# Grouped 3x3 convolution: one weight tile, a longer lag between two pipes, and an early write into the output

## The chip, the cores and the metric

One core of one Trainium2 chip. The metric is the device time of one execution in microseconds (us), as the median of several runs. The profile is of one execution.

## The reference

`x` is 16 x 64 x 64 x 64 (batch, channels, height, width), `weight` is 128 x 8 x 3 x 3, both fp32, with 8 groups. Each group takes 8 input channels to 16 output channels with a 3x3 kernel and zero padding of 1; the output is 16 x 128 x 64 x 64 in fp32.

```python
for g in range(groups):
    for b in range(batch):
        for co in range(16):
            for ci in range(8):
                for kh in range(3):
                    for kw in range(3):
                        output[b, g*16 + co] += weight[g*16 + co, ci, kh, kw] * \
                            x_pad[b, g*8 + ci, kh:kh+h, kw:kw+w]
```

## The kernel before

**Data.** The 16 x 64 rows (image, channel) of `x` are read in tiles of 128 rows, two images in each. Four tiles `xn0` to `xn3` hold images 0 to 7. Four tiles `xs0` to `xs3` hold images 8 to 15 shifted by 32 rows, so that in `xs` the 32-row blocks of an image stand at other partitions than in `xn`. All of them are bf16. They are loaded by 17 DMAs which GpSimd issues at the start, with a cast from fp32 on the way (`load`, L105). Only rows 0 to 31 of `xn0` come another way: SyncE reads them as fp32 into `raw`, which is the first half of the last output buffer (L116), and ScalarE casts them in two pieces (L121).

**Weights.** `weight` lands in `w_sb` (L118, issued by ScalarE). GpSimd makes a mask of groups and an identity (L136 to L146). VectorE multiplies weights and mask into `E` (5 products, L162); TensorE transposes `E` by 18 products with the identity (L175), 9 with offset 0 and 9 with offset 32; VectorE copies the first nine into `wN`, ScalarE the others into `wS` (L185). A 32x64 piece of these tiles is the block-diagonal weight of four groups for one tap of the 3x3 kernel.

**Two pipes.** Pipe 0 works on `xn` with `wN`, pipe 1 on `xs` with `wS`. Each has 16 sets (`st`): for each of four pairs of images `i`, four sets `s` of 16 image rows. A set has 9 taps; each tap is 8 matmuls of a 32x64 piece of the array (L240), for two images, two halves of the channels and two banks. The first tap is the middle one, the others follow in their order. The order of instructions is written out over slots: a pipe takes one tap in a slot, then rests 3 slots after 9 (`PERIOD` 12). Pipe 1 runs `LAG` 6 slots behind pipe 0, so that always at least one of them has a tap.

**Out.** After a set, `finish` copies four PSUM banks into two output buffers `ob` (L268; ScalarE and VectorE in turn). There are eight buffers of 2 MB, one image in each; a pair of images takes two, pipes in turn, so a pair uses the buffers that the same pipe's pair `i - 2` had, and its first copy waits for that one's stores (`self.empty`). SyncE issues the stores (L278): after the last set of a pair, whole images of 2 MB; for the first pair of both pipes (`i == 0`), halves of 1 MB, one after set 1 and one after set 3.

Of the kernel before, what the change touches and what calls it, by code (L numbers as in the profile page):

```python
# [7 lines left out]
FP32 = mybir.dt.float32  # L8
BF16 = mybir.dt.bfloat16
ALU = mybir.AluOpType  # L10


@with_exitstack
def kernel(
    ctx: ExitStack,
    tc: tile.TileContext,
    x: bass.AP,
    weight: bass.AP,
    groups: int,
    out: bass.AP,  # L20
):
    nc = tc.nc

    B, C, H, W = x.shape
    CO, CIg, K, _ = weight.shape
    G = groups
    COg = CO // G
    HW = H * W
    T = K * K
    assert (B, C, CO, K, G, H, W) == (16, 64, 128, 3, 8, 64, 64)  # L30

    R = 8
    NCH = H // R
    HALF = HW // 2

    NOB = 8

    pool = ctx.enter_context(tc.tile_pool(name="sb", bufs=1))
    psum = ctx.enter_context(tc.tile_pool(name="psum", bufs=1, space=bass.MemoryType.PSUM))

    xn = [pool.tile([128, H, W], BF16, name=f"xn{i}") for i in range(4)]
    xs = [pool.tile([128, H, W], BF16, name=f"xs{i}") for i in range(4)]
    ob = [pool.tile([128, HW], FP32, name=f"ob{i}") for i in range(NOB)]
    w_sb = pool.tile([128, CIg * T], FP32, name="w_sb")
    mask = pool.tile([128, G], FP32, name="mask")
    ident = pool.tile([128, 128], BF16, name="ident")
    E = pool.tile([128, T, 160], BF16, name="E")
    wN = pool.tile([128, T, 128], BF16, name="wN")
    wS = pool.tile([128, T, 128], BF16, name="wS")
    banks = [psum.tile([128, 512], FP32, name=f"bank{i}") for i in range(8)]  # L50

    with tc.tile_critical():  # L52
        program(nc, x, weight, out, xn, xs, ob, w_sb, mask, ident, E, wN, wS, banks)


class Order:
# [23 lines left out]
        return self.sem, self.n  # L80


def program(nc, x, weight, out, xn, xs, ob, w_sb, mask, ident, E, wN, wS, banks):
    H = W = 64
    HW, HALF, T, G, CIg, COg, R = H * W, H * W // 2, 9, 8, 8, 16, 8
    NOB = len(ob)
# [7 lines left out]
    def sem(name):  # L94
        s = nc.alloc_semaphore(name)
        sems.append(s)
        return s
# [13 lines left out]
                landed[t.name, q, h] = (s, 16)  # L111


    raw = ob[NOB - 1][:, 0:HALF]
    s_raw = sem("raw")
    nc.sync.dma_start(raw, xr[0:128, 0:HALF]).then_inc(s_raw, 16)  # L116
    s_w = sem("w")
    nc.scalar.dma_start(w_sb, weight.rearrange("co ci kh kw -> co (ci kh kw)")).then_inc(s_w, 16)  # L118
    ACT.wait((s_raw, 16))
    for h in (0, 16):  # L120
        raw_read = ACT.done(nc.scalar.copy(  # L121
            xn[0][:, h : h + 16, :].rearrange("p h w -> p (h w)"), raw[:, h * W : (h + 16) * W],
        ))
        for q in range(4):
            for r in range(h, h + 16):
                landed[xn[0].name, q, r] = raw_read

    m1 = DVE.done(nc.vector.memset(mask, 1.0))  # L128
    m2 = DVE.done(nc.vector.memset(ident, 0.0))  # L129
    for h0, h1 in ((0, 32), (32, 64)):  # L130
        if h0 > 0:
            load(xn[0], 0, 0, 128, h0, h1)
        load(xs[0], 544, 0, 128, h0, h1)
        if h0 == 0:
            POOL.wait(m1)
            m3 = POOL.done(nc.gpsimd.affine_select(  # L136
                out=mask, in_=mask, compare_op=ALU.is_ge, fill=0.0,
                base=0, channel_multiplier=1, pattern=[[-COg, G]],
            ))
            POOL.wait(m2)  # L140
            m4 = POOL.done(nc.gpsimd.affine_select(  # L141
                out=ident, in_=ident, compare_op=ALU.not_equal, fill=1.0,
                base=0, channel_multiplier=1, pattern=[[-1, 128]],
            ))
            POOL.wait(m3)
            m5 = POOL.done(nc.gpsimd.affine_select(  # L146
                out=mask, in_=mask, compare_op=ALU.is_ge, fill=0.0,
                base=COg - 1, channel_multiplier=-1, pattern=[[COg, G]],
            ))
        load(xs[3], 512 - 96, 96, 128, h0, h1)  # L150
    for i in range(1, 4):
# [3 lines left out]

    wv = w_sb.rearrange("co (ci t) -> co t ci", t=T)
    DVE.wait((s_w, 16), m5)
    for r in range(5):  # L160
        g0 = 4 * (r % 2)
        e = DVE.done(nc.vector.tensor_mul(  # L162
            E[:, :, 32 * r : 32 * r + 32].rearrange("p t (g c) -> p t g c", c=CIg),
            wv.unsqueeze(2).to_broadcast([128, T, 4, CIg]),
            mask[:, g0 : g0 + 4].unsqueeze(1).unsqueeze(3).to_broadcast([128, T, 4, CIg]),
        ))
    PE.wait(e, m4)
    free = [None] * 8
    w_need = {}
    for k, (wt, off) in enumerate(((wN, 0), (wS, 32))):  # L170
        for g, t0 in enumerate(range(0, T, 4)):
            n = min(4, T - t0)
            b = 4 * k + g
            for t in range(n):
                ins = nc.tensor.matmul(  # L175
                    banks[b][:, 128 * t : 128 * t + 128],
                    E[:, t0 + t, off : off + 128],
                    ident,
                    start=True, stop=True,
                )  # L180
            p = PE.done(ins)
            dst = wt[:, t0 : t0 + n, :].rearrange("p t c -> p (t c)")
            eng, copy = ((DVE, nc.vector.tensor_copy), (ACT, nc.scalar.copy))[k]
            eng.wait(p)
            free[b] = eng.done(copy(dst, banks[b][:, 0 : 128 * n]))  # L185
            for t in range(n):
                w_need[wt.name, t0 + t] = free[b]

    outf = out.rearrange("b co h w -> b co (h w)")
    taps = [(1, 1)] + [(a, b) for a in range(3) for b in range(3) if (a, b) != (1, 1)]
    pe = nc.tensor
    stored = [nc.alloc_semaphore(f"st{i}") for i in range(NOB)]
    uses = [0] * NOB
    nob = [0]
# [2 lines left out]
    class Pipe:  # L200
# [5 lines left out]
        def streams(self, i):  # L206

            if self.k == 0:
                return [(q // 2, wN, xn[i], q, q % 2) for q in range(4)]
            return [  # L210
                (0, wS, xs[i], 0, 1), (1, wS, xs[i], 1, 0),
                (1, wS, xs[i], 2, 1), (0, wS, xs[i - 1], 3, 0),
            ]

        def matmuls(self, st, k, j):
# [6 lines left out]
            v0 = w0 - (kw - 1)  # L222
            nr, nw = hi - lo, w1 - w0
            left = {0: 2, 1: 2}
            for im, wt, xt, q, half in self.streams(i):
                b = self.banks[j][im]
                pos = dict(tile_position=(32 * q, 64 * half))
                w_ap = wt[32 * q : 32 * q + 32, 3 * kh + kw, 64 * half : 64 * half + 64]
                x_ap = xt[32 * q : 32 * q + 32, lo:hi, w0:w1]
                o_ap = banks[b].rearrange("p (h w) -> p h w", w=W)[  # L230
                    64 * half : 64 * half + 64, o0 : o0 + nr, v0 : v0 + nw
                ]
                if j == 0:
                    PE.wait(w_need[wt.name, 3 * kh + kw])
                    pe.ldweights(w_ap, **pos)  # L235
                PE.wait(
                    free[b] if k == 0 else None,
                    landed[xt.name, q, lo], landed[xt.name, q, hi - 1],
                )
                ins = pe.add_instruction(  # L240
                    mybir.InstMatmult(
                        name=nc.get_next_instruction_name(),
                        engine=mybir.EngineType.PE,
                        start_tensor_calc=k == 0, stop_tensor_calc=k == T - 1,
                        tile_size=(32, 64), ldweights=False, **pos,
                        ins=[pe.lower_ap(x_ap, opt=False), pe.lower_ap(w_ap, opt=False, for_matmul_weights=True)],
                        outs=[pe.lower_ap(o_ap)],
                    )
                )
                left[im] -= 1  # L250
                if k == T - 1 and left[im] == 0:
                    self.full[j, im] = PE.done(ins)

        def finish(self, st):
            i, s = st // 4, st % 4
            if s == 0:
                self.slots = [(nob[0] + im) % NOB for im in range(2)]
                self.empty = [(stored[slot], 16 * uses[slot]) if uses[slot] else raw_read for slot in self.slots]
                self.wrote = [[], []]
                nob[0] += 2  # L260
            for j in range(2):
# [7 lines left out]
                    self.wrote[im].append(free[b])  # L269
                nev[0] += 1  # L270
            nev[0] += 1
            if s == 1 and i == 0 or s == 3:
                o0, o1 = (0 if s == 1 or not (i == 0) else HALF), HALF * (s + 1) // 2
                for im in range(2):
                    slot = self.slots[im]
                    img = 2 * i + 8 * self.k + im
# [2 lines left out]
                    uses[slot] += 1  # L279

    pipes = (Pipe(0), Pipe(1))
    PERIOD, LAG, NSETS = T + 3, (T + 3) // 2, 16
    for slot in range(PERIOD * NSETS + LAG):
        live = []
        for p, lag in zip(pipes, (0, LAG)):
# [60 lines left out]
```

## Time and profile before

| | |
|---|---|
| median of 10 runs | 128.52 us (128.32 to 128.94) |
| the profiled execution, own time | 128.49 us |
| its span (first to last recorded event) | 126.8 us |
| TensorE matmul busy | 87.1 us (69%) |
| VectorE, ScalarE, GpSimd busy | 46.0, 39.0, 9.9 us |
| bytes read from and written to memory | 16.81 MB, 33.55 MB |
| stores of an image, of a half | 12 of 2048 KB, 8 of 1024 KB |

The span leaves out 1.7 us of the execution's own time. In a table of windows, a row is a stretch of the span: its bounds, its length, each engine's busy time, the TensorE clock, the DMA share (mean busy share of the 16 DMA engines, over 1 where packets of two queues overlap on an engine) and the GB/s that landed. A load with a cast counts there with the bf16 bytes that it writes, which is half of what it reads.

### The profile page before, as it was taken

The page shows a single profiled execution, that of the slowest core. Times are in us where ns is not written, and L with a number is a line of the kernel's source. Part 1 is how long each engine was busy: PE and PEld are TensorE (multiplying, and loading weights), DVE is VectorE, ACT ScalarE, POOL GpSimd, SP SyncE. Part 2 cuts the span into 40 slices and gives each one's busy share as a digit, 9 for nine tenths or more (in the row PEclk, how much of TensorE's full clock was granted, in tenths as well). Part 3 has the DMA queues.
Part 4 walks back from the last instruction along what each step waited for, and adds up shares of the span by engine and source line. Part 5 has one row for each costly group of instructions (what it writes and reads, how often), then busy time and mean ns, then how long its engine had stood idle before and what let it go on. Part 6 is the DMA issues. An engine that isn't in the chain of part 4 may idle for free.

```text
span 126.8 us, 3785 instructions
## 1 busy us (share of the span) xinstructions
PE 87.1 (69%) x2322; PEld 39.9 (31%) x1170; DVE 46.0 (36%) x74; ACT 39.0 (31%) x70; POOL 9.9 (8%) x24
## 2 busy tenths in 40 slices
PE   0029999999999999997539999999999700000000
PEld 0024435445444554551114446443363200000000
DVE  0273065456445544444224654555446500000000
ACT  4063153345335433341033633426335400000000
POOL 5995000000000000000000000000000000000000
PEclk9999999999999999999999999999999995555555
DMA  2999999999999999999999999999999999999960
GB/s 47 349 209 208 220 213 207 211 282 310 319 314 308 330 302 321 318 313 314 408 426 421 429 434 424 419 429 424 424 429 424 424 429 445 424 429 439 419 279 10
DMA packets 5375, 42.74 MB, mean 337 GB/s; under 512 B 752, under 2 KB 752, under 8 KB 2672
## 3 DMA queue, kind: packets, MB, share of 16 engines
q1 hardware_dynamic: 3024, 34.60, 65.2%
q0 software_dynamic: 2192, 7.87, 31.1%
q8 instruction: 13, 0.21, 0.6%
q10 hardware_dynamic: 144, 0.04, 0.2%
q14 instruction: 2, 0.02, 0.0%
HBM read 16.81 MB, written 33.55 MB: 397 GB/s over the span
## 4 chain that ended last, share of the span: by engine, by line
PE 45%; DMA 27%; DVE 5%; issue 1%; ACT 0%; SPq 0%; ACTq 0%; DVEq 0%
PE bank L240 44%; DMA out_dram<-ob 24%; DMA w_sb<-in_weight_dram 4%; DVE ob L268 3%; DVE E L162 2%; PE bank L175 2%; ACT ob L268 0%; ACTq L341 0%; DVEq L74 0%; SPq L278 0%; SPq L52 0%
## 5 line engine op out<-in xcount | busy, mean ns | idle before, releaser
L240 PE MATMUL bank<-xs,wS 32*64 32x504 bf16 (+3 forms) x1152 | 72.0, 373 | 3.6 <-ACT ob L268 1.9
L240 PE MATMUL bank<-xn,wN 32*64 32x504 bf16 (+3 forms) x1152 | 71.2, 377 | 1.1 <-DVE ob L268 1.1
L268 DVE COPY ob<-bank 128x512 f32<-128x512 f32 x64 | 41.4, 686 | 49.4 <-PE bank L240 41.7
L268 ACT COPY ob<-bank 128x512 f32<-128x512 f32 x64 | 34.5, 589 | 55.4 <-PE bank L240 45.6
L235 PEld LDWEIGHTS <-wS 32*64 32x64 bf16 x576 | 26.2, 104 | 23.6 <-issue 13.8
L235 PEld LDWEIGHTS <-wN 32*64 32x64 bf16 x576 | 19.3, 105 | 27.7 <-issue 23.0
L175 PE MATMUL bank<-ident,E 128*128 128x128 bf16 x18 | 2.1, 310 | 8.6 <-DVE E L162 8.6
L105 POOL DMA_DIRECT2D xs<-in_x_dram x10 | 5.9, 591 | 1.0 <-SPq L52 1.0
L175 PEld LDWEIGHTS bank<-ident,E 128*128 128x128 bf16 x18 | 1.8, 143 | 8.6 <-DVE E L162 8.6
L162 DVE TENSOR_TENSOR E<-w_sb,mask 128x288 bf16<-128x288 f32 x5 | 2.9, 651 | 4.4 <-DMA w_sb<-in_weight_dram 4.4
L105 POOL DMA_DIRECT2D xn<-in_x_dram x7 | 4.2, 601 | 0.0
L121 ACT CAST xn<-ob 128x1024 bf16<-128x1024 f32 x2 | 2.0, 1044 | 3.9 <-DMA ob<-in_x_dram 3.9
L185 ACT CAST wS<-bank 128x512 bf16<-128x512 f32 (+1 forms) x3 | 1.2, 487 | 1.7 <-PE bank L175 1.7
L185 DVE CAST wN<-bank 128x512 bf16<-128x512 f32 (+1 forms) x3 | 1.5, 551 | 0.7 <-PE bank L175 0.7
L121 ACT ACT_TABLE_LOAD x1 | 1.3, 1283 | 1.4 <-SPq L52 1.4
L128 DVE MEMSET mask<- 128x8 f32 x1 | 0.1, 65 | 1.1 <-SPq L52 1.1
L141 POOL TENSOR_SCALAR_AFFINE_SELECT ident<-ident 128x128 bf16<-128x128 bf16 x1 | 0.3, 304 | 0.0
L136 POOL TENSOR_SCALAR_AFFINE_SELECT mask<-mask 128x8 f32<-128x8 f32 x1 | 0.2, 211 | 0.1
L146 POOL TENSOR_SCALAR_AFFINE_SELECT mask<-mask 128x8 f32<-128x8 f32 x1 | 0.2, 199 | 0.0
L327 POOL MEMSET const-float32-0.0<- 128x1 f32 x1 | 0.1, 99 | 0.3 <-issue 0.3
L129 DVE MEMSET ident<- 128x64 uint32 x1 | 0.1, 112 | 0.0
L327 POOL MEMSET const-bfloat16-1.0<- 128x1 bf16 x1 | 0.1, 103 | 0.0
(2 smaller groups left out, 0.2 us busy)
## 6 DMA issues: line engine op xcount, KB each, us to landing
out_dram<-ob SPq DMA_DIRECT2D x12, 2048.0 KB, 19.9
out_dram<-ob SPq DMA_DIRECT2D x8, 1024.0 KB, 21.9
xn<-in_x_dram POOLq DMA_DIRECT2D x7, 512.0 KB, 24.0
xs<-in_x_dram POOLq DMA_DIRECT2D x6, 512.0 KB, 17.2
ob<-in_x_dram SPq DMA_DIRECT2D x1, 1024.0 KB, 5.5
xs<-in_x_dram POOLq DMA_DIRECT2D x2, 384.0 KB, 49.0
xs<-in_x_dram POOLq DMA_DIRECT2D x2, 128.0 KB, 9.1
w_sb<-in_weight_dram ACTq DMA_DIRECT2D x1, 36.0 KB, 4.7
```

Source lines behind the costliest of these rows:

```text
L105: nc.gpsimd.dma_start(t.rearrange("p h w -> p (h w)")[p0:p1, h0 * W : h1 * W], xr[row0 + p0 : row0 + p1, h0 * W : h1 * W],).then_inc(s, 16)
L121: raw_read = ACT.done(nc.scalar.copy(xn[0][:, h : h + 16, :].rearrange("p h w -> p (h w)"), raw[:, h * W : (h + 16) * W],))
L136: m3 = POOL.done(nc.gpsimd.affine_select(out=mask, in_=mask, compare_op=ALU.is_ge, fill=0.0, base=0, channel_multiplier=1, pattern=[[-COg, ...
L141: m4 = POOL.done(nc.gpsimd.affine_select(out=ident, in_=ident, compare_op=ALU.not_equal, fill=1.0, base=0, channel_multiplier=1, pattern=[ ...
L146: m5 = POOL.done(nc.gpsimd.affine_select(out=mask, in_=mask, compare_op=ALU.is_ge, fill=0.0, base=COg - 1, channel_multiplier=-1, pattern= ...
L162: e = DVE.done(nc.vector.tensor_mul(E[:, :, 32 * r : 32 * r + 32].rearrange("p t (g c) -> p t g c", c=CIg), wv.unsqueeze(2).to_broadcast([ ...
L175: ins = nc.tensor.matmul(banks[b][:, 128 * t : 128 * t + 128], E[:, t0 + t, off : off + 128], ident, start=True, stop=True,)
L185: free[b] = eng.done(copy(dst, banks[b][:, 0 : 128 * n]))
L235: pe.ldweights(w_ap, **pos)
L240: ins = pe.add_instruction(mybir.InstMatmult(name=nc.get_next_instruction_name(), engine=mybir.EngineType.PE, start_tensor_calc=k == 0, st ...
L268: free[b] = eng.done(copy(ob[slot][:, o0 : o0 + 512], banks[b]))
L327: nc = _bacc.Bacc("TRN2", target_bir_lowering=False, num_devices=1)
```

## The change

1. One weight tile `wt` takes the place of `wN` and `wS`. VectorE first spreads the weights over all 16 blocks of 8 columns in `wb` (3 copies), TensorE transposes (9 products), and VectorE multiplies by a mask of 128x4 on the way out of PSUM (3 products). The mask is built as 128x4x4 and summed to 128x4 by one reduction. The taps come in another order: 4, 5, 6, 7, 0, 1, 2, 3, 8.
2. `raw` is read in two DMAs (image rows 0 to 7, then 8 to 31) and cast in four pieces of 8 rows.
3. ScalarE issues one more DMA at the start: 16 rows of 512 B of `x` are written into output image 15. That image is overwritten later; SyncE waits for this DMA ahead of its first store.
4. Pipe 1 runs 18 slots behind pipe 0, not 6.
5. Of the first pairs, only pipe 0's is stored in halves; pipe 1's is stored as whole images.

```diff
-    raw = ob[NOB - 1][:, 0:HALF]
-    s_raw = sem("raw")
-    nc.sync.dma_start(raw, xr[0:128, 0:HALF]).then_inc(s_raw, 16)
+    raw = ob[NOB - 1]
     s_w = sem("w")
     nc.scalar.dma_start(w_sb, weight.rearrange("co ci kh kw -> co (ci kh kw)")).then_inc(s_w, 16)
-    ACT.wait((s_raw, 16))
-    for h in (0, 16):
-        raw_read = ACT.done(nc.scalar.copy(
-            xn[0][:, h : h + 16, :].rearrange("p h w -> p (h w)"), raw[:, h * W : (h + 16) * W],
-        ))
...
+    s_warm = sem("warm")
+    outf = out.rearrange("b co h w -> b co (h w)")
+    nc.scalar.dma_start(outf[15][0:16, 0:128], xr[0:16, 0:128]).then_inc(s_warm, 16)
+    raw_read = []
+    for h0, h1 in ((0, 8), (8, 32)):
+        s_raw = sem(f"raw{h0}")
+        nc.sync.dma_start(raw[:, h0 * W : h1 * W], xr[0:128, h0 * W : h1 * W]).then_inc(s_raw, 16)
+        for h in range(h0, h1, 8):
+            ACT.wait((s_raw, 16))
+            raw_read = [ACT.done(nc.scalar.copy(
+                xn[0][:, h : h + 8, :].rearrange("p h w -> p (h w)"), raw[:, h * W : (h + 8) * W],
+            ))]
...
+    taps = [(t // 3, t % 3) for t in (4, 5, 6, 7, 0, 1, 2, 3, 8)]
+    DVE.wait(m5)
+    r = DVE.done(nc.vector.tensor_reduce(
+        out=mask, in_=mask4.rearrange("p q g -> p g q"), op=ALU.add, axis=mybir.AxisListType.X,
+    ))
+    DVE.wait((s_w, 16))
     wv = w_sb.rearrange("co (ci t) -> co t ci", t=T)
-    DVE.wait((s_w, 16), m5)
-    for r in range(5):
-        g0 = 4 * (r % 2)
-        e = DVE.done(nc.vector.tensor_mul(
...
+    groups = ((0, 4, 4), (4, 0, 4), (8, 8, 1))
+    filled = [DVE.done(nc.vector.tensor_copy(
+        wb[:, k0 : k0 + n, :].rearrange("p t (g c) -> p t g c", c=CIg),
+        wv[:, t0 : t0 + n, :].unsqueeze(2).to_broadcast([128, n, 16, CIg]),
+    )) for k0, t0, n in groups]
+    PE.wait(m4)
+    free = [None] * 8
+    w_need = []
+    for b, (k0, t0, n) in enumerate(groups):
+        PE.wait(filled[b])
+        for k in range(n):
+            ins = nc.tensor.matmul(
+                banks[b][:, 128 * k : 128 * k + 128], wb[:, k0 + k, :], ident, start=True, stop=True,
+            )
+        p = PE.done(ins)
+        DVE.wait(p, r)
+        free[b] = DVE.done(nc.vector.tensor_mul(
+            wt[:, k0 : k0 + n, :].rearrange("p t (h g c) -> p (t h) g c", h=2, g=4),
+            banks[b][:, 0 : 128 * n].rearrange("p (t g c) -> p t g c", g=4, c=COg),
+            mask.unsqueeze(1).unsqueeze(3).to_broadcast([128, 2 * n, 4, COg]),
         ))
...
+        w_need += [free[b]] * n
...
+    SP.wait((s_warm, 16))
...
-            if s == 1 and i == 0 or s == 3:
-                o0, o1 = (0 if s == 1 or not (i == 0) else HALF), HALF * (s + 1) // 2
+            if s == 1 and i + self.k == 0 or s == 3:
+                o0, o1 = (0 if s == 1 or not (i + self.k == 0) else HALF), HALF * (s + 1) // 2
...
-    PERIOD, LAG, NSETS = T + 3, (T + 3) // 2, 16
+    PERIOD, LAG, NSETS = T + 3, (T + 3) // 2 + T + 3, 16
```

## The prediction

> **What bounds the kernel now.** I read the page's slices first, then its list of DMA issues, then the waits, then a table of windows.
>
> ```profile
> PE   0029999999999999997539999999999700000000
> PEclk9999999999999999999999999999999995555555
> DMA  2999999999999999999999999999999999999960
> ```
>
> The DMA engines are busy from the second slice to the last but one; TensorE stops at about 101 us and 25 us of stores follow. So TensorE is not the end's cause. The waits say the same:
>
> ```profile
> ACT ob L268 <- DMA out_dram<-ob: 9.9, 3, 6.6
> DVE ob L268 <- DMA out_dram<-ob: 7.7, 3, 3.6
> PE bank L240 <- DVE ob L268: 2.6, 4, 1.5
> PE bank L240 <- ACT ob L268: 1.9, 1, 1.9
> ```
>
> The copies out of PSUM wait for stores (second figure: times), and TensorE waits for those copies. No row has a matmul waiting for an `xn` or `xs` load. The windows then give the rate of the DMA engines, stage by stage (last column GB/s landed):
>
> ```profile
> 2.00:3.00 1.00, 0.00 (x0) 0.00 (x0) 0.00 (x0) 0.69 (x1) 0.91 (x5) 1.00 0.49 76
> 3.00:4.00 1.00, 0.00 (x0) 0.00 (x0) 0.00 (x0) 0.00 (x0) 1.00 (x3) 1.00 1.03 345
> ...
> 16.00:22.00 6.00, 5.82 (x164) 2.66 (x87) 3.41 (x6) 2.71 (x6) 0.00 (x0) 1.00 1.07 215
> ...
> 24.00:25.50 1.50, 1.50 (x64) 0.85 (x24) 0.36 (x1) 0.11 (x1) 0.00 (x0) 1.00 1.14 202
> 25.50:27.00 1.50, 1.50 (x48) 0.77 (x20) 1.29 (x2) 1.07 (x2) 0.00 (x0) 1.00 0.98 248
> ...
> 33.00:60.00 27.00, 26.01 (x731) 11.96 (x360) 12.89 (x20) 10.84 (x20) 0.00 (x0) 1.00 1.04 316
> 66.00:80.00 14.00, 13.96 (x408) 6.63 (x205) 6.68 (x11) 5.65 (x11) 0.00 (x0) 1.00 1.01 426
> ...
> 102.00:120.00 18.00, 0.00 (x0) 0.00 (x0) 0.00 (x0) 0.00 (x0) 0.00 (x0) 0.58 1.01 432
> 120.00:122.00 2.00, 0.00 (x0) 0.00 (x0) 0.00 (x0) 0.00 (x0) 0.00 (x0) 0.50 0.86 369
> 122.00:123.00 1.00, 0.00 (x0) 0.00 (x0) 0.00 (x0) 0.00 (x0) 0.00 (x0) 0.50 0.54 229
> ```
>
> From 16 to 22 us there are casting loads alone: 215 GB/s landed is 430 read. From 33 to 60 us loads and stores share the engines: the packet records give 104 landed by loads and 210 by stores, so 2 x 104 + 210 = 418 on the memory side. From 66 us stores alone run at 426. All stages stand at 418 to 432: whatever the order of the work, the engines do about 0.42 MB in a us. 16.81 MB read and 33.55 MB written at 0.42 are 120 us; with about 3 us before the engines fill and 1.6 us after the last packet (125.2 us) that is the span. Only three places lie below the rate: the head (2 to 4 us); 24 to 27 us, where the first stores begin; and the tail (120 to 125 us), where some engines have finished and others have not.
>
> The dip at 24 to 27 us matters most here. The first store is issued at 22.0 us, its first packet is recorded only at 25.6 (the first read was issued at 1.0 and its packet is at 2.1), and load packets beside it take 0.44 to 0.76 us in place of 0.32. Against 215 and 316 GB/s the two windows miss (215 - 202) x 1.5 / 215 = 0.1 us and (316 - 248) x 1.5 / 316 = 0.3 us, together 0.4 us of all engines. The other images, with addresses of their own, show no such dip (33 to 60 us is even).
>
> **The change part by part.**
>
> *Weights.* Removed: 5 products of 0.65 us (L162), 9 of 18 transposes (18 take 2.1 us), the casts into `wS` (1.2 us of ScalarE). Added: 3 spreading copies, one small reduction, 3 products out of PSUM. The nearest row to a 512-element copy is `L185` on VectorE at 0.69 us; the strided source could make it 0.65 x 512/288 = 1.15. The first matmul now waits for weights (5.6 us), one copy (0.7 to 1.15), 4 transposes (0.5) and one product (0.7): 7.5 to 8.0 us in place of 10.7, if `raw` rows 8 to 15 are cast by then. The groups for later taps come behind on VectorE (two copies, then two products, about 2 us), so one short stall is likely: 2 to 3 us earlier in all, I take 2.5. The reduction waits for the mask (GpSimd ends at 2.85 us), before the weights land: nothing. The DMA engines have loads queued until about 64 us, and these hide all of this. On the end: 0. GpSimd issues the same DMAs behind the same three selects.
>
> *Lag 18.* A slot is 0.42 us (the half store after slot 20 is issued at 22.0, the one after slot 44 at 32.0). TensorE's last set comes 12 slots later, +5.0 us, less 2.5 for the early start and less some of the roughly 6 us of buffer stalls: last store issued between 98 and 104 us against 101.8. The DMA queue holds work to 125 and needs only 2 x 4.85 us for the last two images, so TensorE could be some 11 us later still before it set the end. The other stores: all that is queued before pair `i = 2` (loads and four pairs, 33.6 MB) lasts the engines from 3 to 83 us; pipe 0's pair 2 is issued near 72 to 76 (78.4 now). The next pair is due by 93 and comes by 84, the next by 103 and comes by 95. Each has 7 us or more of cover. With fewer stores early, loads go no later at first, but from about 41 us whole images in 16 KB packets take turns with 8 KB load packets, so loads end near 75 us and not 64; the last rows of `xn3` come near 72, first used in slot 158, 7.8 + 66 = 74 us. Tight, and a stall of 2 us there costs nothing by the cover above. On the end: 0; without that cover each us of it is a us.
>
> *Whole images for pipe 1's first pair.* Per DMA engine, 32 packets of 8 KB (0.322 us by the packet records) become 16 of 16 KB (0.611). That is 16 x (2 x 0.322 - 0.611) = 0.5 us if packets run one behind the other, and with the overlap in the DMA share (1.04 against 1.01) 16 x (0.644 / 1.04 - 0.611 / 1.01) = 0.2 us. I take -0.2 (ends -0.5 and 0). Against it, loads are mixed with stores for some 11 us longer, at 418 where loads alone have 430 and stores 426: up to 0.25 us, I take +0.1.
>
> *raw in two DMAs.* 8 packets of 8 KB per engine become 8 of 2 KB and 8 of 6 KB. From the two packet sizes, 0.033 us of each packet doesn't depend on its bytes, so 8 x 0.033 = 0.26 us at most, and 0 where packets overlap; the row 3 to 4 us is below full rate anyway. I take +0.1. The page DMA: Bandwidth & Descriptors of the Trainium skill (Anatomy of one DMA) speaks harder against this and the early write: 2.0 us fixed for each DMA, plus its bytes at 436 GB/s, and its Rules for kernel authors call transfers under 64 KB mostly overhead. Two more DMAs would be +4 us, two fewer stores -4. The trace denies that the fixed part adds up in a full queue: the last two stores,
>
> ```profile
> L278 SPq DMA_DIRECT2D out_dram<-ob x2: 333/428/523, 101.5 to 101.8; - x2
> DMA to landing us min/median/max: 19.3/21.6/23.8
> ```
>
> land at 120.8 and 125.6, 4.8 us apart, and 2.10 MB at 432 GB/s are 4.85. I count packets alone. ScalarE has 0.41 us more of issuing and 4 casts (about 0.6 us each, by the copy of 512 elements in L268) for 2 of 1.04: hidden as above.
>
> *The early write.* 16 packets of 512 B, one per engine, bytes negligible. SyncE's wait for it stands ahead of the first store near 19 us and is long over. If the dip belongs to the first write into the output tensor, it is paid at the start. No row shows such a write. Its gain is at best the whole dip, -0.4, if it is paid while the engines stand half idle (2 to 3 us, share 0.49); at worst it stalls the head by as much, and the dip stays: +0.4. Weights go ahead of it in ScalarE's queue, so it falls partly on the full engines from 3 us on. I take -0.3, nearest to the dip's own row, as no later image has a dip.
>
> Sum: -0.3 - 0.2 + 0.1 + 0.1 = -0.3 us on 128.49, which is 128.2; the median stands 0.03 above the profiled execution. A measurement of this kernel can hardly tell less than 0.2% (0.26 us) from no change, so this lies just beyond it. One term I can't forecast: at the end the slowest engine finishes 3.8 us after the fastest. The completion packets put this at 1.5 us when the mixed stage ends (64 us), and steps of 0.5 to 1.0 follow instruction fetches of 16 KB (72, 91, 97 us), each a detour of one engine. Which engine is hit may change with the program: 0 with ends of 0.6 either way.
>
> **The rivals.**
>
> A. As forecast, or better with a luckier spread of the fetches: 127.6 to 128.25. For it: the dip, and that it comes once. Chance 0.50.
>
> B. The dip is moved, not removed: the early write costs the head what it saves at 24 us. The DMA bytes are the same, and packets and longer mixing cancel: 128.5. For it: the head already has slow first packets (0.6 to 1.3 us) and full engines from 3 us. Chance 0.25.
>
> C. Slower: the dip belongs to the start of a store from the output buffers, not to the tensor's first write. Then the early write stalls the head (+0.4), nothing is saved later, and small `raw` packets add 0.1 to 0.26: 128.49 + 0.6 = 129.1. It decides when the dip after the first store keeps more than half of its 0.4 us. Chance 0.17.
>
> D. The engines run dry: pipe 1's pairs come so late that the store queue empties. It takes over 7 us of delay in TensorE beyond my schedule, say by late `xn3` rows; every us beyond is one: about 130. Chance 0.08.
>
> **How the numbers follow.** Faster by over 0.2% is A, 0.50; within is B, 0.25; slower is C and D, 0.25. The predicted time is A's, 128.2. The range leaves out D and the edges: 127.4 (A with the packet gain of 0.5 and 0.5 of luck in the spread) to 129.1 (C). A's own range is 127.6 to 128.25.
>
> **What would show it.** Right: no rate below 300 GB/s as the first stores start, near 20 to 25 us, and a shorter time from first issue to first packet; first convolution matmul near 8 us; last store issue at 98 to 104 us; DMA share 9 in each slice; loads landing until about 75 us. Wrong: a window with DMA share under 0.9 between 10 and 118 us (D), a dip as deep as before after the first store (C), or a head that fills later than 4 us (B). The last packet's time against the middle engine's tells the fetches' share.

## The result, and the profile after

The changed kernel takes 127.69 us in the median of 9 runs (127.53 to 127.80), against 128.65 for the kernel before in the runs beside it: ratio 0.9925, interval 0.9912 to 0.9937. The profiled execution took 127.67 us (before 128.49), its span is 125.9 us. So it is faster by about 0.75%, where 0.25% was forecast.

The page's slices look as before: the DMA engines are full from the second slice on, TensorE still ends at 101 us.

```profile
PE   0299799999999999998998999997997910000000
PEclk9999999999999999999999999999999996555555
DMA  3999999999999999999999999999999999999981
```

The copies out of PSUM wait much less for stores (4.0 us in place of 17.6):

```profile
DVE ob L273 <- DMA out_dram<-ob: 3.0, 1, 3.0
...
ACT ob L273 <- DMA out_dram<-ob: 1.0, 1, 1.0
```

That would matter only if TensorE set the end. The windows (start and end, length, busy time of TensorE, weight loads, VectorE, ScalarE, GpSimd, clock, DMA share, GB/s landed) show what the DMA engines did:

```profile
2.00:3.00 1.00, 0.00 (x0) 0.00 (x0) 0.06 (x1) 0.94 (x1) 0.91 (x5) 1.00 0.82 214
3.00:4.00 1.00, 0.00 (x0) 0.00 (x0) 0.12 (x1) 0.34 (x1) 1.00 (x3) 1.00 1.05 310
...
16.00:20.00 4.00, 3.99 (x114) 1.63 (x56) 1.20 (x2) 1.07 (x2) 0.00 (x0) 1.00 1.07 214
...
21.50:24.50 3.00, 3.00 (x90) 1.50 (x46) 1.90 (x4) 1.54 (x4) 0.00 (x0) 1.00 1.01 165
24.50:27.00 2.50, 2.50 (x84) 1.26 (x37) 1.17 (x3) 1.10 (x3) 0.00 (x0) 1.00 1.04 328
```

The dip at the first store is not gone. It is deeper: 165 GB/s for 3 us where 214 would be the rate of loads alone, (214 - 165) x 3 / 214 = 0.7 us, against 0.4 before. The first store is issued at 20.0 us and its first packet is recorded at 24.2.

The other difference is late:

```profile
60.00:70.00 10.00, 9.39 (x275) 4.15 (x136) 5.16 (x8) 4.29 (x8) 0.00 (x0) 1.00 1.03 356
70.00:76.00 6.00, 6.00 (x176) 2.19 (x86) 2.58 (x4) 2.15 (x4) 0.00 (x0) 1.00 1.01 383
80.00:100.00 20.00, 18.43 (x452) 6.86 (x223) 8.36 (x14) 6.99 (x13) 0.00 (x0) 1.00 1.00 424
```

A figure under 424 here means that casting loads still run (they land half of what they read). Before, 66 to 76 us was at 428:

```profile
66.00:76.00 10.00, 9.96 (x289) 4.43 (x144) 5.09 (x8) 4.30 (x8) 0.00 (x0) 1.00 1.01 428
```

Now 70 to 76 us is at 383. The loads end at 74.9 us by the packet records, before at 62.7. The list of DMA issues has it too (size, median us to landing; before, these two took 49.0):

```profile
xs<-in_x_dram POOLq DMA_DIRECT2D x2, 384.0 KB, 58.7
```

And the tail is shorter (two rows of before, then three of now):

```profile
123.00:124.00 1.00, 0.00 (x0) 0.00 (x0) 0.00 (x0) 0.00 (x0) 0.00 (x0) 0.50 0.23 98
124.00:125.00 1.00, 0.00 (x0) 0.00 (x0) 0.00 (x0) 0.00 (x0) 0.00 (x0) 0.50 0.04 16
```
```profile
122.00:123.00 1.00, 0.00 (x0) 0.00 (x0) 0.00 (x0) 0.00 (x0) 0.00 (x0) 0.50 0.46 197
123.00:124.00 1.00, 0.00 (x0) 0.00 (x0) 0.00 (x0) 0.00 (x0) 0.00 (x0) 0.50 0.34 147
124.00:125.00 1.00, 0.00 (x0) 0.00 (x0) 0.00 (x0) 0.00 (x0) 0.00 (x0) 0.50 0.00 0
```

From 124 us on the share is 0.00, where it was 0.04 (16 GB/s, one engine still storing). The packet records show when each engine ends, though they do not number the engines. Each DMA ends with one 4-byte packet on each of 16 engines; for the last store these stand, in us after the fastest engine:

```
before: 0 .11 .12 .33 .33 .48  1.12 1.22 1.25 1.51  2.07 2.57 2.75 2.75 2.79 3.78   fastest 121.38, mean 122.83, last 125.16
after:  0 .03 .38 .39 .50 .67  .94 1.22 1.27 1.45   1.91 2.46 2.60 2.67 2.72 2.80   fastest 121.65, mean 123.02, last 124.45
```

The mean engine ends 0.2 us later than before. The last one ends 0.7 us earlier. The gain lies wholly in the distance from the mean engine to the last, 2.33 us before and 1.43 now.

**Where that distance comes from.** Two things hold back single engines. First, TensorE's instructions are fetched in 16 KB packets, 13 in each kernel, and each makes one engine about 1.25 us late (in the mixed stage, where nothing else moves the engines against each other, one of them steps by 1.25 us with each fetch). By the groups near 0.3, 1.2 and 2.7 in the lists, some engines have none, some one and some two. Second, from about the end of the loads until TensorE ends, there is one unbroken chain of slow store packets. Each starts where the last ended, so they are one engine's:

```
before, start us / took us: 66.15 .662 | 66.81 .688 | 67.49 .662 | 68.16 .680 | 68.83 .686 | ... | 99.47 .644 | 100.11 .653 | 100.77 .633
the other 16 KB store packets: .611 to .618 but for six of .96 to 1.02, five of them right behind an instruction fetch;  after 104 us all of them .611 to .618
```

In 34.6 us this engine loses 3.9 us, 0.11 us in each us. The completion packets of the earlier stores let one follow it: it stands 0.06 us after the fastest engine at 63 us, 0.84 at 73, 2.1 at 82, 3.2 at 92, 3.77 at 102, and 3.78 in every store after that. So the slow engine is the last one. In the changed kernel the chain begins at 73.1 us and its engine ends 2.60 us after the fastest; the last one there, at 2.80, is another. While casting loads run beside the stores, no engine stands out in this way: 8 KB store packets are at 0.322 us up to the 95th percentile in both kernels, and 16 KB ones beside loads at 0.624.

**Theory M**, formed after the first four runs: whole images in 16 KB packets leave loads in 8 KB packets a smaller share of each engine (packets of stores and loads come out equal in number: 537 and 531 from 39 to 60 us before, both of 8 KB; 353 and 361 from 48 to 69 us now), so loads last longer, the stage in which one engine is slow is shorter, and the last engine ends nearer to the others. Rivals: the early write pays (W), the lag pays (L), the fixed cost of packets (P), or only luck with the fetches (F). Theory S, in the first four, says no more than that the gain is in the spread of the engines.

### The profile page after: what moved, and what is told of

It reads as the page before. It is cut to its first block, busy times and chain, and to the rows that moved or that the text cites. A ratio compares the mean times of both kernels' runs of the same rounds, so it can differ in the third digit from the quotient of the medians.

```text
span 125.9 us, 3765 instructions
## 1 busy us (share of the span) xinstructions
PE 91.2 (72%) x2313; PEld 36.8 (29%) x1161; DVE 44.4 (35%) x73; ACT 38.0 (30%) x69; POOL 9.9 (8%) x24
## 4 chain that ended last, share of the span: by engine, by line
PE 49%; DMA 25%; DVE 6%; issue 1%; SPq 0%; ACTq 0%; DVEq 0%
PE bank L245 48%; DMA out_dram<-ob 22%; DVE ob L273 5%; DMA w_sb<-in_weight_dram 3%; DVE wt L188 1%; DVE wb L173 0%; PE bank L183 0%; SPq L283 0%; ACTq L346 0%; DVEq L74 0%; SPq L74 0%; SPq L52 0%
## 5 line engine op out<-in xcount | busy, mean ns | idle before, releaser
L245 PE MATMUL bank<-xn,wt 32*64 32x504 bf16 (+3 forms) x1152 | 73.8, 383 | 2.0 <-issue 1.0
L245 PE MATMUL bank<-xs,wt 32*64 32x504 bf16 (+3 forms) x1152 | 70.6, 373 | 2.4 <-DVE ob L273 1.1
L240 PEld LDWEIGHTS <-wt 32*64 32x64 bf16 x1152 | 36.0, 105 | 58.1 <-issue 45.2
L183 PE MATMUL bank<-ident,wb 128*128 128x128 bf16 x9 | 1.2, 306 | 5.5 <-DVE wb L173 5.5
L127 ACT CAST xn<-ob 128x512 bf16<-128x512 f32 x4 | 2.3, 616 | 3.2 <-DMA ob<-in_x_dram 3.2
L183 PEld LDWEIGHTS bank<-ident,wb 128*128 128x128 bf16 x9 | 0.8, 131 | 5.6 <-issue 5.4
L173 DVE CAST wb<-w_sb 128x512 bf16<-128x512 f32 (+1 forms) x3 | 1.4, 501 | 1.6 <-DMA w_sb<-in_weight_dram 1.6
L188 DVE TENSOR_TENSOR wt<-bank,mask 128x512 bf16<-128x512 f32 (+1 forms) x3 | 1.5, 552 | 0.0
```

The source lines that it names most:

```text
L127: raw_read = [ACT.done(nc.scalar.copy(xn[0][:, h : h + 8, :].rearrange("p h w -> p (h w)"), raw[:, h * W : (h + 8) * W],))]
L173: filled = [DVE.done(nc.vector.tensor_copy(wb[:, k0 : k0 + n, :].rearrange("p t (g c) -> p t g c", c=CIg), wv[:, t0 : t0 + n, :].unsqueeze ...
L183: ins = nc.tensor.matmul(banks[b][:, 128 * k : 128 * k + 128], wb[:, k0 + k, :], ident, start=True, stop=True,)
L188: free[b] = DVE.done(nc.vector.tensor_mul(wt[:, k0 : k0 + n, :].rearrange("p t (h g c) -> p (t h) g c", h=2, g=4), banks[b][:, 0 : 128 * n ...
L245: ins = pe.add_instruction(mybir.InstMatmult(name=nc.get_next_instruction_name(), engine=mybir.EngineType.PE, start_tensor_calc=k == 0, st ...
```

## The experiments

Distances are from the mean engine's end to the last engine's end in the one profiled run of each row. "Chain loses" adds up what the chain's packets above 0.63 us take beyond 0.611 until TensorE ends (a narrower count than the 3.9 us above).

| kernel | ratio to before (interval) | first store issued | loads end | chain loses | mean engine | last engine | distance |
|---|---|---|---|---|---|---|---|
| before | 1 | 22.0 | 62.7 | 3.8 | 122.83 | 125.16 | 2.33 |
| before, lag 18 | 1.0017 (0.9997 to 1.0036) | 21.5 | 62.9 | 3.8 | 122.76 | 125.58 | 2.82 |
| before, new weights | 0.9991 (0.9982 to 1.0000) | 20.0 | 64.7 | 3.8 | 122.87 | 125.08 | 2.21 |
| after, all first pairs in halves | 0.9986 (0.9977 to 0.9995) | 19.1 | 66.9 | 3.4 | 122.97 | 125.00 | 2.03 |
| after, no early write (again) | 0.9925 (0.9906 to 0.9944) | 22.4 | 70.5 | 3.3 | 122.97 | 124.77 | 1.80 |
| before, whole images for pipe 1 | 0.9951 (0.9938 to 0.9964) | 21.8 | 70.6 | 3.5 | 122.65 | 124.52 | 1.87 |
| after (again) | 0.9920 (0.9901 to 0.9938) | 22.0 | 70.7 | 3.1 | 122.98 | 125.36 | 2.39 |
| after, no early write, one raw DMA | 0.9915 (0.9894 to 0.9936) | 22.2 | 71.0 | 3.2 | 122.78 | 124.78 | 2.00 |
| after, one raw DMA | 0.9960 (0.9940 to 0.9980) | 21.0 | 73.4 | 3.0 | 122.85 | 124.53 | 1.68 |
| after | 0.9925 (0.9912 to 0.9937) | 20.0 | 74.9 | 2.6 | 123.02 | 124.45 | 1.43 |
| after, no early write | 0.9945 (0.9933 to 0.9958) | 20.4 | 75.0 | 2.8 | 123.00 | 124.41 | 1.41 |
| after, lag 6 | 0.9945 (0.9929 to 0.9962) | 19.0 | 79.1 | 2.5 | 123.26 | 124.57 | 1.31 |
| before, small last loads | 0.9926 (0.9910 to 0.9942) | 21.9 | 80.5 | 2.5 | 123.28 | 124.61 | 1.33 |

The rows stand in the order of the loads' end. What the chain loses falls in nearly the same order; the distance follows it with exceptions of up to half a us (after, again). The three profiles whose loads end at 70.5, 70.7 and 71.0 us are of the slowest run of their kernels, 0.3 to 0.9 us above the median, so their ends go less well with the ratios beside them. The loads' end itself goes with two things: whole images or halves, and, within each, how early the first store is issued (whole images: 19.0 us goes with 79.1, 22.4 with 70.5; small loads apart).

**Without the early write.**

```diff
-    s_warm = sem("warm")
-    nc.scalar.dma_start(outf[15][0:16, 0:128], xr[0:16, 0:128]).then_inc(s_warm, 16)
-    SP.wait((s_warm, 16))
```

> The changed kernel without the early write of x into output image 15 (and without SyncE's wait for it). In the trace of the changed kernel the dip as the first stores start is still there, and no smaller (about 0.8 us of all DMA engines at 21.5 to 24.2 us, against 0.5 before). Theory S (the gain is in the spread between the DMA engines at the end, not in the bytes or the dip): 127.7 us, within 0.3, and the dip at the first store stays between 0.5 and 0.9 us of lost time. Rival W (the early write pays for the gain): 128.4 to 128.6 us, and a deeper dip or a later first packet of a store.

Measured: 127.84 us. The dip is the same without it:

```profile
21.50:24.50 3.00, 3.00 (x94) 1.57 (x43) 1.66 (x3) 1.26 (x3) 0.00 (x0) 1.00 1.05 160
```

160 GB/s against 165 with it. The early write doesn't touch what it was thought to touch. The ratio left 0.2% open, so the pair was run once more, below.

**The changed kernel with lag 6.**

```diff
-    PERIOD, LAG, NSETS = T + 3, (T + 3) // 2 + T + 3, 16
+    PERIOD, LAG, NSETS = T + 3, (T + 3) // 2, 16
```

> The changed kernel with pipe 1 at lag 6 again; all else as changed, so pipe 1's first pair is stored as whole images. Theory S: the DMA engines stay full, the median engine ends at 122.6 to 122.9 us as in both kernels, and the time moves only with which engines the instruction fetches and late packets hit: 127.4 to 128.7, no side preferred. Rival L (the lag is what gains, because ScalarE, VectorE and TensorE wait less for buffers): 128.4 to 128.7, with the buffer waits back at 10 us or more.

Measured: 127.85 us. Most of the gain is there without the lag, although the waits of the copies for stores are back (15.8 us), so L fails as the cause. But this is the one kernel whose DMA engines did run dry, as the last stores were issued at 104.4 and 104.8 us:

```profile
102.00:104.00 2.00, 1.42 (x27) 0.43 (x8) 0.69 (x2) 0.72 (x2) 0.00 (x0) 1.00 0.83 352
```

A share of 0.83 for 2 us is 0.2 to 0.3 us of all engines. The difference of 0.2% to the changed kernel may be that, though the intervals overlap; and since the pause brought the engines nearer together (3.09 us from the fastest to the slowest ahead of it, 2.24 behind), the short distance of this row is not M's alone.

**The changed kernel with one raw DMA.**

```diff
-    for h0, h1 in ((0, 8), (8, 32)):
+    for h0, h1 in ((0, 32),):
```

> The changed kernel with raw read by one DMA of 1 MB, still cast in four pieces. Theory S: 127.7 us within 0.4; the spread of the engines when raw has landed goes back to about 0.9 us from 1.9. Rival H (the head fills sooner with the split): 128.0 to 128.2. By the packet sizes it could also gain up to 0.26 us: 127.4.

Measured: 127.97 us, 0.996 (0.994 to 0.998). Taken alone this speaks for H, a head that fills sooner: 2 to 3 us is at 214 GB/s with the split, at 76 in the kernel before. But it is at 173 here with one DMA, so most of that is not the split's. And the mean engine ended at 122.85 us, no later than with the split; the dip was smaller (188 GB/s from 22.5 to 25.5 us). The run without both (below) decides.

**The kernel before with lag 18.**

```diff
-    PERIOD, LAG, NSETS = T + 3, (T + 3) // 2, 16
+    PERIOD, LAG, NSETS = T + 3, (T + 3) // 2 + T + 3, 16
```

> The kernel before with pipe 1 at lag 18 and nothing else changed. TensorE starts at 10.7 us as before, so its last store is issued near 104 us, still 11 us before the engines would want it. Theory S: 128.6 within 0.6, the median engine unchanged; whichever way the time goes, the end of the slowest engine less that of the median one goes the same way by the same amount. Rival L (the lag gains): 127.7 to 128.0. Rival D (pipe 1 is too late): 129 or more with a gap in the DMA share.

Measured: 128.91 us, 1.0017 (0.9997 to 1.0036). The lag gains nothing by itself. TensorE's last matmuls start at 102.3 us in place of 100.1, the loads end where they did, and the last engine stands 4.32 us after the fastest, not 3.78. This made the slow chain visible: the stage is longer by 2 to 3 us, so by theory 0.3 us more would be lost in it; its packets add up to only 0.1 us more, and the rest of the difference is where the engine stood when the stage began.

**The kernel before with pipe 1's first pair in whole images.**

```diff
-            if s == 1 and i == 0 or s == 3:
-                o0, o1 = (0 if s == 1 or not (i == 0) else HALF), HALF * (s + 1) // 2
+            if s == 1 and i + self.k == 0 or s == 3:
+                o0, o1 = (0 if s == 1 or not (i + self.k == 0) else HALF), HALF * (s + 1) // 2
```

> The kernel before with pipe 1's first pair stored as whole images; nothing else changed. Theory M: in the traces so far one DMA engine has store packets of 0.64 to 0.73 us in place of 0.61, in an unbroken chain from the time the loads end until TensorE ends, and so falls behind by about 0.11 us each us; that engine is the last to finish. Whole images in 16 KB packets take a larger share of each DMA engine beside the 8 KB load packets, so the loads end later (near 75 us, not 63), the slow stage is 12 us shorter, and the last engine ends 1.0 to 1.3 us nearer to the others: 127.3 to 127.9, with the spread down from 3.8 to about 2.8. Rival P (the gain is in the packets' fixed cost): 128.0 to 128.4 with the mean engine 0.2 to 0.5 us earlier and the same spread. Rival F (only the luck of which engine takes the instruction fetches): anywhere from 127.5 to 129, with no link to the loads' end.

Measured: 128.07 us, 0.9951 (0.9938 to 0.9964). This one condition brings two thirds of the whole gain. The loads take longer (before: 49.0 us), and the window after 60 us still has loads in it:

```profile
xs<-in_x_dram POOLq DMA_DIRECT2D x2, 384.0 KB, 55.8
```
```profile
60.00:70.00 10.00, 7.08 (x161) 2.05 (x74) 3.14 (x5) 3.22 (x6) 0.00 (x0) 0.83 1.03 365
70.00:76.00 6.00, 6.00 (x177) 2.94 (x89) 2.71 (x5) 2.15 (x4) 0.00 (x0) 1.00 1.01 427
```

It came less far than expected: loads end at 70.6 us, not 75, the distance falls by 0.46, not over 1. P may have a part: the mean engine ends 0.18 us earlier, the 0.2 us that the forecast gave to larger packets. That is one profile; the changed kernels with whole images have it at 122.78 or later, no earlier than the kernels with halves.

**The changed kernel with both first pairs in halves.**

```diff
-            if s == 1 and i + self.k == 0 or s == 3:
-                o0, o1 = (0 if s == 1 or not (i + self.k == 0) else HALF), HALF * (s + 1) // 2
+            if s == 1 and i == 0 or s == 3:
+                o0, o1 = (0 if s == 1 or not (i == 0) else HALF), HALF * (s + 1) // 2
```

> The changed kernel with both pipes' first pairs stored in halves, as before. Theory M: loads end near 63 us again, the slow stage lasts from there to about 102, the spread is back at 3.8 to 4.3: 128.4 to 129.0, so nearly the whole gain is gone. Rival P: 127.9 to 128.2, the mean engine later and the spread as in the changed kernel.

Measured: 128.50 us, 0.9986 (0.9977 to 0.9995). New weights, lag, split and early write all remain, and the gain is nearly gone. M had expected loads near 63 us and a spread of 3.8 to 4.3; they end at 66.9, as the first store is issued 2.9 us earlier than before, and the spread is 3.45.

**The kernel before with the new weights alone** (part 1 of the change, with its order of taps).

```diff
-    for r in range(5):
-        e = DVE.done(nc.vector.tensor_mul(E[:, :, 32 * r : 32 * r + 32]...
+    filled = [DVE.done(nc.vector.tensor_copy(wb[:, k0 : k0 + n, :]...
```

> The kernel before with the new weight build alone (one tile, new order of taps). TensorE starts near 8 us, but the loads end where they did. Theory M: the slow stage can only be shorter by what TensorE ends earlier, 0 to 2.5 us, so 0 to 0.3 us: 128.2 to 128.6. Rival F: up to 0.7 either way. If an early start of TensorE were the cause: 127.7.

Measured: 128.55 us, 0.9991 (0.9982 to 1.0000). An earlier TensorE is worth next to nothing, as forecast.

**Five of nine taps**, to ask what the slow engine depends on.

```diff
-                p.matmuls(st, k, j)
+                if k not in (1, 2, 3, 4):
+                    p.matmuls(st, k, j)
```

> The kernel before with 5 of 9 taps: the matmuls and weight loads of taps 1 to 4 are left out, so 1280 matmuls and 640 weight loads run in place of 2304 and 1152; copies out of PSUM, loads and stores are all as before. The DMA bytes don't change. If the slow engine comes from TensorE's stream of instructions (matmuls and weight loads), the extra on its store packets falls from about 0.075 us a packet to near half, 7 or 8 instruction fetches take the place of 13, and the time is 127.0 to 127.8. If it comes from the copies out of PSUM or from the stores themselves, the extra stays at 0.06 to 0.08 us a packet and the time is 128.0 to 128.6.

Measured: 127.07 us, 0.9876 (0.9858 to 0.9895), with the same loads, copies and stores but for the shorter instruction stream. The row of the instruction queue (packets, MB, share) falls from 13 packets to 7:

```profile
q8 instruction: 13, 0.21, 0.6%
...
q8 instruction: 7, 0.11, 0.3%
```

The mean engine ends at 122.35 us: six fetches of 1.25 us spread over 16 engines are 0.47 us, the slow engine's smaller loss is 0.1 more, and 0.48 is measured. No engine is in the group near 2.7 but the slow one (2.79). The slow chain is still there and weaker, 2.3 us from 68.5 to 98.5 us, 0.08 in each us in place of 0.11; matmuls and weight loads run at 468 in 80 to 100 us in place of 808:

```profile
80.00:100.00 20.00, 19.92 (x541) 8.89 (x267) 10.16 (x16) 8.31 (x16) 0.00 (x0) 1.00 1.01 426
...
80.00:100.00 20.00, 13.50 (x320) 4.32 (x148) 11.49 (x18) 9.61 (x18) 0.00 (x0) 1.00 1.01 428
```

So the slowness falls with TensorE's stream, if less than in proportion (0.7 of the rate at 0.58 of the instructions), and not with the copies out of PSUM (18 on each engine here, 16 before). The run with lag 6 agrees from within: while TensorE stands nearly still, its chain loses 0.02 us in 3 us, in place of about 0.3.

```profile
84.00:87.00 3.00, 0.42 (x7) 0.13 (x2) 0.69 (x1) 1.06 (x2) 0.00 (x0) 0.73 1.01 431
```

**The kernel before with small last loads.** This sets M against P: smaller packets, more of them, and stores untouched.

```diff
-        for h0, h1 in ((0, 32), (32, 64)):
+        for h0, h1 in ((0, 32), (32, 64)) if i < 3 else ((0, 16), (16, 32), (32, 48), (48, 64)):
```

> The kernel before with the four last loads (xn3, xs3) split into eight of 16 image rows each, so that a packet of theirs reads 4 KB and not 8 KB; same bytes, stores as before in 8 KB and 16 KB packets. Theory M (the slow stage of one DMA engine begins when the loads end): in turns with store packets of 8 KB the last loads get a smaller share, so they end 4 to 8 us later (67 to 71 us), and the last engine ends 0.4 to 0.9 us less behind the mean one; some 50 more packets for each engine cost the mean up to 0.4 us: 127.9 to 128.4, and the spread from the fastest to the slowest engine below 3.3. Rival P (the packets' fixed cost alone makes the gain of the whole images): smaller packets can only cost: 128.8 to 129.1.

Measured: 127.92 us, 0.9926 (0.9910 to 0.9942): the whole gain of the change, from splitting four loads. The mean engine ends 0.45 us later, so the small packets do cost something; the distance to the last falls by 1.0, and the fastest-to-slowest spread is 2.51 us. Its windows show loads until 80 us:

```profile
66.00:76.00 10.00, 10.00 (x285) 4.20 (x136) 3.90 (x7) 3.30 (x7) 0.00 (x0) 0.95 1.04 381
76.00:80.00 4.00, 4.00 (x120) 1.93 (x55) 2.54 (x4) 2.06 (x4) 0.00 (x0) 1.00 1.00 401
```

P would have this kernel slower than before. M holds in an edit that shares nothing with the change but the later end of the loads: the chain loses 2.5 us, and its engine is no longer the last. The loads' end was missed by far (67 to 71 us expected).

**The changed kernel without early write and split, and the pair again.** The first is the edit of both runs above together; the other two are the changed kernel and the one without the early write.

> The changed kernel without the early write and with raw read by one DMA: the new weights, the lag of 18 and whole images for pipe 1 remain. If the early write and the split of raw are worth something each, as the two runs without one of them say (0.2 and 0.35 percent above the changed kernel), this one is at 128.1 to 128.3. If they are worth nothing together, 127.6 to 127.8; the dip at the first store was smallest in kernels with one raw DMA (0.3 to 0.6 us against 0.9), which speaks for 127.5.

> The changed kernel once more, beside the next run on the same chip. 127.6 to 127.9 by every theory; it is here for the comparison.

> The changed kernel without the early write once more, on the same chip as the changed kernel. Theory W (the early write is worth 0.2 us or more): 0.15 to 0.3 us slower than the run beside it. Otherwise within 0.1 us of it.

Measured: 127.72 us (ratio 0.9915, 0.9894 to 0.9936) without both; 127.80 (0.9920, 0.9901 to 0.9938) for the changed kernel; 127.86 (0.9925, 0.9906 to 0.9944) without the early write. All three are one result. Neither the early write nor the split of `raw` is worth anything that can be measured here; the 0.2 and 0.35% of the first runs did not come back.

The profiled run of the changed kernel was this time its slowest, 128.68 us, and it supports M in part and shows its limit. Its first store was issued at 22.0 us and not 20.0, so stores began to take turns later, its loads ended at 70.7 us and not 74.9, and its last engine ended at 125.36 us, 3.94 us after the fastest; the mean engine ended at 122.98, as in the other run (123.02). The chain lost 3.1 us in place of 2.6; the other 0.8 us of the 3.94 is how far its engine was behind already when the chain began, where in the kernel before it was 0.06. So with loads that end 8 us later than before, this distance is no smaller (2.39 against 2.33): M says what the slow engine loses, not where it starts.

```profile
xs<-in_x_dram POOLq DMA_DIRECT2D x2, 384.0 KB, 54.5
```

## Why the prediction was right, and where it was not

*What bounds the kernel.* Right: the DMA engines are full from the head to the tail in every kernel of the table but the one with lag 6 (share 0.83 for 2 us), and about 0.42 MB a us stands in all of them.

*Weights and lag on the end: 0.* Right, alone (0.9991, 1.0017); in the changed kernel the lag may be worth up to 0.2%, since without it the engines run dry for a moment. The first convolution matmul came at 6.8 us, earlier than the forecast 7.5 to 8.0, because the weights landed sooner (3.7 us after the issue in place of 4.7). The last store was issued at 102.4 us, within the 98 to 104 that were given.

*Early write: -0.3.* This step failed. The dip does not belong to the first write into the output tensor: it is 0.7 us in the changed kernel with the early write or without. Rival C had said that too, but the head was not stalled either, so nothing was paid: its +0.4 failed as well. The worth of the write is 0 within 0.2 us. Without this term the forecast's sum is 0, so that it said faster, and the right way, is luck. What the dip is was not found; it stands at the first store in all kernels, it began 1.5 to 3 us after that store's issue and ended when the first store packets ran.

*raw in two DMAs: +0.1.* It is 0 together with the early write. At 2 to 3 us the head fills faster (214 GB/s, 173 with one raw DMA, 76 before) rather than slower, and the dip is deeper (165, 188 with one raw DMA); what makes the head faster and whether the two belong together is open. The fit of 2.0 us for each DMA that the prediction quotes is given on its page for DMAs that GpSimd issues; here it was held against SyncE's and ScalarE's.

*Whole images: -0.2.* Alone they measured -0.18 for the mean engine, in one profile; it did not show again in the changed kernel, so as a cost of packets this is not settled.

*Longer mixing: +0.1.* The loads were forecast to end near 75 us and did (74.9; 70.7 in the second profile, where the first store came 2 us later). The step's cost is real for the mean engine (0.2 us later in the changed kernel, 0.45 with small loads). But the same later end was the gain, and the working didn't see it.

*The spread of the engines: 0, ends of 0.6.* This is the term that was mis-sized, and it was -0.9. It was taken for luck with the instruction fetches. The fetches are there, but of the steps that the prediction gave to them, those near 91 and 97 us are the slow engine's, which falls behind by 0.5 us in each 4.9 us from store to store. The engine that ends last before the change was held back by a steady loss that runs only between the loads' end and TensorE's, and the change shortens that stage from both the larger store packets and the earlier first store. Where the slow engine stands when the stage begins is still luck (0.06 and 0.8 us). Sum of the terms as measured: +0.2 for the mean engine, -0.9 for the distance to the last, -0.7 for the last packet (125.16 to 124.45), and 0.1 less behind it. So the direction was right, the number about a third of what came, and the cause that it named was the wrong one.

What stays open: what TensorE's stream puts on that one DMA engine, and why casting loads beside the stores hide it. The page DMA: Bandwidth & Descriptors of the Trainium skill (Latency and other measured facts) lists two of 16 engines as usually slower, with contention from GpSimd's descriptor rings as best guess. These runs don't agree for this case: one engine is slow, and only once GpSimd's loads are over; the packet records don't say which one. The parts also don't add up fully: whole images (-0.5%) and weights (-0.1%) leave 0.2% of the 0.8% to their joint effect, probably the earlier first store: the table's loads end later with it, but it was not tried by itself. And each kernel has one profile, or two, so the ends of single engines are known for one execution, the medians for all.

No version that takes all nine taps was faster than the changed kernel beyond the intervals. The changed kernel without early write and split (0.9915) does as well with fewer instructions. Small loads in the changed kernel were not tried: its last engines are already those with two fetches (2.5 to 2.8 us after the fastest), which a still shorter slow stage would not move.

## What to carry to other kernels

When the DMA engines are the bound and always full, ask not only for their mean rate but which one ends last: compare the completion packets of the last DMA over the 16 engines, and the DMA share in the tail's windows. Bytes and mean time can stay equal, or get worse, while the end moves by 1%. And when a part has a reason that sounds good (an early write against a dip), look in the next profile for the dip itself before crediting it.

## What was not expected of the hardware

- The two queues put out packets in equal number, so the size of a packet sets its queue's share (537 to 531 with both at 8 KB, 353 to 361 with stores at 16, 502 to 502 with loads at 4): beside 8 KB load packets, stores in 16 KB packets made the loads end 8 us later (62.7 to 70.6); halving the packets of the last loads made them end 18 us later (80.5).
- One 16 KB fetch of TensorE's instructions makes one DMA engine 1.25 us late, about two 16 KB store packets; 13 fetches put 2.7 us between the engines' ends, 7 fetches 1.65 (the slow engine aside).
- One DMA engine's store packets take 0.63 to 0.73 us in place of 0.61 while TensorE runs and no casting loads do.
- Eight loads in place of four, with half the packet size, made the kernel faster, though the mean engine ended 0.45 us later; that is all that four more DMAs and their smaller packets cost in a full queue.
